# One block product of the values in the head, kept in HBM, and the second chunk of projections whole

## The chip, the cores and the metric

The kernel runs on one core of a Trainium2 chip. Its time is the device time of one execution in microseconds (us); a kernel's figure is the median of several runs. The program is float32 throughout: every product is made of three matrix products of parts in fp32r (the operand is split into a high part and a low part, and high x high, high x low and low x high are added up in one PSUM bank). The engines are PE (matrix products and transposes), ACT, DVE and POOL (elementwise work), and SP, which here only issues transfers.

## The reference

One layer for 512 tokens of 1024 features:

```
xn = RMSNorm(x);  u = xn @ W_in          # columns: q | k | v | rnn_x | rnn_gate | gate_A | gate_B
ya = chunked_band_attention(q, k, v) @ W_attn_out       # 16 heads of 64, chunks of 64, 9 chunks in reach
xc = causal_conv4(rnn_x);  hr = rg_lru(xc)              # two block-diagonal gates, a scan over the tokens
yb = (hr * gelu(rnn_gate)) @ W_rnn_out
h  = x + (sigmoid(gate_A) * ya + sigmoid(gate_B) * yb) @ W_o
h  = h + (silu(g) * up) @ W_ffn_out,  (g | up) = RMSNorm(h) @ W_ffn_in;  out = RMSNorm(h)
```

What the change touches is `rnn_gate` for the first 256 features (chunk `gr0` of `W_in`) and the values `v = xn @ W_v`.

## The kernel before, in words

**Chunks.** The projections run over chunks of 256 columns of `W_in` (`xr0`, `gr0`, `ga0`, `gb0`, `xr2` and so on: rnn_x, rnn_gate, gate_A, gate_B), each for all 512 tokens, as two column tiles of 128 (c = 0, 1) by 8 feature blocks (k = 0 to 7) by three matrix products. A chunk's weights come as two raw tiles of 512 KB (feature blocks 0 to 3 and 4 to 7), and ACT makes the high part (L86, or L670 in the head) and DVE the low part (L87, L671) into tiles named `whl_...`. Raw tiles have three buffers, `whl` tiles four; a new tile waits until the one before it in its buffer has been read for the last time. `prefetch` makes the next chunk's parts in the order of the list `chunks`.

**The head.** The head works in two halves of the tokens. For the first half, DVE and ACT scale the rows, PE transposes them (`turned`, L652, tiles `pt_mix...`), ACT and DVE make the high and the low part of `xnT`, and PE makes the first half of the tokens of `xr0` (`first_half`, products of 128x256) as the blocks arrive. Then comes a fill: the first half of the tokens of `gr0`. While PE works on it, ACT and DVE scale the second half's rows. Then the second half's transposes follow, and with them the second half of the tokens of `xr0` and of `gr0`. Here the order on ACT, DVE and POOL is the order of the code; the order on PE and of the transfers is chosen by a scheduler when the program is built, and fixed then.

**The values.** `v_all` makes the values as a 2 x 2 block product in seven products instead of eight: halves of the tokens by halves of the features, with sums of weight blocks (`t1` to `t4`) and of token blocks (`s1` to `s4`). Each product is 2 banks by 4 feature blocks by 3, so 24 matrix products of 128x512. `x_`, `z_` and `y_` are pairs of PSUM banks. On PE the order is that of the code: `w11` into `x_`, `t1` into `z_`, `t2` onto `x_`, `w22` onto `z_`, `t3` onto `x_`, `w21` into `y_`, `t4` onto `x_`. In between, ACT copies bank contents to SBUF (`keep`, L1025), DVE adds a bank to a kept sum (`summed`, L1035), and ACT and DVE split the sum into the tiles that attention reads (`given`). `t4` = `w21` minus the second sum of weights; it is made when `w21` comes (L310). ACT and DVE here take the scheduler's order.

Of the kernel before, what the change touches and what calls it, by code (L numbers as in the profile page):

```python
# [8 lines left out]
F32 = mybir.dt.float32  # L9
# [5 lines left out]
P = 128  # L15
D = 1024
S = 512
# [25 lines left out]
def block_kernel(ctx: ExitStack, tc: tile.TileContext, x, norm_mix_g, w_in, b_merge, rel_table,  # L43
# [68 lines left out]

    v_groups = ((0, 3), (1, 2))

    v_kinds = ("w11", "t1", "t2", "w22", "t3", "w21", "t4")
    plan_qk(0)
    plan_qk(1)
    for j in range(0, KT, 2):
# [11 lines left out]
        plan(f"o_{kind}")  # L130
    f_units = [f"f{w}{n}" for n in range(3) for w in "gu"]
    f_first = ("w11", "w21", "t4", "t1", "t2", "w22", "t3")
    for unit in f_units:
        for kind in f_first if unit == f_units[0] else v_kinds:
            plan(f"{unit}_{kind}")

    plain, paired = list(range(N_PLAIN)), list(range(N_PLAIN, FT // 2))
# [24 lines left out]
    def load(name, k):  # L162
        _, parts, rows, kts = chunks[index[name]]
        wide = sum(width for *_, width in parts)
        n = min(4 * CW // wide, kts - k)
        at = rows + k * P
        raw = out_raw_home(name) if name[:2] == "fo" else wp.tile([P, n, wide], F32, tag="raw", bufs=3, name=f"raw_{name}_{k}")
        to = 0
        for src, col, width in parts:
            sp.dma_start(out=raw[:, :, to:to + width],  # L170
                         in_=src[at:at + n * P, col:col + width].rearrange("(k p) e -> p k e", p=P))
            to += width
        raws[name, k] = raw
# [122 lines left out]
    def v_weights(kind):  # L296

        hl = [wp.tile([P, 2, 2, S], F32R, tag="whl", bufs=4, name=f"whl_v_{kind}_{u}") for u in range(2)]
        for u in range(2):
            if kind == "t1":  # L300
                src = v_t1[u]
            elif kind in ("t2", "t4"):
                src = v_t2[u]
            elif kind == "t3":
                src = v_raw(kind, 0, 0, u)
                tc.keep_in_program_order(dve.tensor_sub(src, v_t2[u], src))
            else:
                src = v_raw(kind, int(kind[1]) - 1, int(kind[2]) - 1, u)
                if kind == "w21":
                    dve.tensor_sub(v_t2[u], src, v_t2[u])  # L310
            split(hl[u][:, 0], hl[u][:, 1], src)
        return lambda part, k: hl[k // 2][:, part, k % 2]

# [174 lines left out]
    load("xr0", 4)  # L488
    for t in range(2, NT):
        sp.dma_start(out=xt[t][:], in_=x[t * P:(t + 1) * P, :])  # L490
    load("gr0", 0)

    wrg_raw = nm.tile([P, 8, 2, 64], F32, name="wrg_raw")
    for n, w in enumerate((w_rg_r, w_rg_i)):
# [185 lines left out]
    def first_half(name, ks):  # L680
        for c in range(2):
            if (name, c) not in first:
                first[name, c] = mm_tile(f"po_{name}_{c}")
        for k in ks:
            for c in range(2):
                at = slice(c * P, (c + 1) * P)
                whl = made[index[name]]
                mm3(first[name, c][:, 0:256], whl(0, k, at), whl(1, k, at),
                    xnT[k][:, 0, 0:256], xnT[k][:, 1, 0:256], k == 0, k == KT - 1)


# [7 lines left out]
    with tc.manual_schedule(engines={mybir.EngineType.Activation, mybir.EngineType.DVE, mybir.EngineType.Pool}):  # L699
        xs, rs = scaled_first(0)  # L700
        xr0 = chunk_in_parts("xr0")
        xr0(0, 2, dve)
        act.copy(gm[:], gm_p[:, 0:8])
        turned(0, xs, 0)
        first_half("xr0", range(0, 2))
        scaled_rest(0, xs, rs)
        xr0(2, 2, dve)
        turned(0, xs, 2)
        first_half("xr0", range(2, 4))
        xr0(4, 2, dve)  # L710
        turned(0, xs, 4)
        first_half("xr0", range(4, 6))
        gr0 = chunk_in_parts("gr0")
        xr0(6, 2, dve)
        turned(0, xs, 6)
        first_half("xr0", range(6, 8))
        gr0(0, 4, dve)
        first_half("gr0", range(0, 4))
        gr0(4, 4, dve)
        xs, rs = scaled_first(1)  # L720
        gate_weights()
        turned(1, xs, 0)
        first_half("gr0", range(4, 8))
        scaled_rest(1, xs, rs)
        turned(1, xs, 2)
        vectors()
        sp2, spm4 = softplus_neg()
        turned(1, xs, 4)
        turned(1, xs, 6)


    ext = nm.tile([HEADS, 640], F32, tag="junk", bufs=1, name="ext")
# [274 lines left out]

    def v_all(sums):
        out, parted, s, s3 = sums
        x_, y_ = ([mm_tile(f"v_{n}{a}", tag) for a in range(2)] for n, tag in (("x", "mm"), ("y", "t")))  # L1010
        z_ = [mm_tile(f"v_z{a}") for a in range(2)]

        def product(banks, kind, rows, start):
            w = weights(f"v_{kind}")
            for a in range(2):
                for k in range(4):
                    if isinstance(rows, str):
                        hi, lo = (o[:, k, a * P:(a + 1) * P] for o in out[rows])
                    else:
                        hi, lo = (x_block(*rows, part)[:, k, a * P:(a + 1) * P] for part in range(2))  # L1020
                    mm3(banks[a][:], hi, lo, w(0, k), w(1, k), start and k == 0, k == 3, parts=True)

        def keep(o, banks):
            for a in range(2):
                act.activation(o[:, a], banks[a][:], AF.Copy)  # L1025

        def given(half, side, src):
            for a in range(2):
                for n, gr in enumerate(v_groups[side]):
                    v = vs[gr][2 * half + a]  # L1030
                    split(v[:, :, 0::3], v[:, :, 1:3], src(a)[:, n * CW:(n + 1) * CW].rearrange("p (a b d) -> p a b d", a=2, b=2))

        def summed(o, banks, half, side):
            for a in range(2):
                dve.tensor_add(o[:, a], banks[a][:], o[:, a])  # L1035
            for gr in v_groups[side]:
                v_pairs(gr, half)
            given(half, side, lambda a: o[:, a])

        product(x_, "w11", (0, 0), True)  # L1040
        keeps = [rnp.tile([P, 2, 2, S], F32, tag="big", bufs=4, name=f"v_keep{n}") for n in range(2)]
        v_big.append(rnp.tile([P, 2, 2, S], F32R, tag="big", bufs=4, name="v_big"))
        x1, x2, z1 = keeps[0][:, 0], keeps[0][:, 1], keeps[1][:, 0]
        keep(x1, x_)
        product(z_, "t1", "s1", True)
        keep(z1, z_)
        parted("s4", s)
        product(x_, "t2", "s2", False)
        keep(x2, x_)
        parted("s3", s3)  # L1050
        product(z_, "w22", "s4", False)
        summed(x2, z_, 0, 1)
        product(x_, "t3", "s3", False)
        summed(z1, x_, 1, 1)
        product(y_, "w21", (0, 1), True)
        summed(x1, y_, 0, 0)
        product(x_, "t4", (1, 1), False)
        for gr in v_groups[0]:
            v_pairs(gr, 1)
        given(1, 0, lambda a: x_[a][:])  # L1060
# [694 lines left out]
```

## Time and profile before

| | |
|---|---|
| median of 3 runs | 845.96 us (845.82 to 846.02) |
| profiled execution | 846.07 us, span 844.3 us, so 1.77 us lie outside the span |
| PE busy | 836.0 us of the span (99%) |
| DVE, ACT, POOL busy | 657.9, 521.5, 152.4 us |
| stage of the head (start of the span to the first product of `ga0`) | 0 to 36.1 us |
| stage of the values (`w11` to `t4`) | 242.2 to 280.3 us |

In the rows of a timeline the first number is the start, the second the duration, and a bracket gives the engine's idle time before and what ended it. Neighbouring matrix products overlap in the record, so what one costs in a row of them is the distance between starts. Names in the rows have lost their numbers: `po_xr` stands for `xr0` in the head.

### The profile page before, as it was taken

How to read it: one execution, taken by the hardware profiler on the slowest of the kernel's cores; microseconds unless marked ns; L12 is line 12 of the kernel's file. 1: busy time of each engine (PE TensorE's matmuls, PEld its weight loads, DVE VectorE, ACT ScalarE, POOL GpSimd, SP SyncE). 2: the span in 40 equal slices, each digit the busy share in tenths (PEclk: the TensorE clock that was granted, in tenths of full speed). 3: DMA queues.
4: the chain of work that ended last, by engine and by line, in shares of the span. 5: the costliest groups of instructions: out<-in, count | busy, mean ns of one | idle time of the engine just before them, and what ended most of it. 6: DMA issues, size and time to landing. Idle time of an engine off the chain costs nothing.

```text
span 844.3 us, 11949 instructions
## 1 busy us (share of the span) xinstructions
PE 836.0 (99%) x4246; PEld 708.5 (84%) x4246; DVE 657.9 (78%) x960; ACT 521.5 (62%) x862; POOL 152.4 (18%) x207
## 2 busy tenths in 40 slices
PE   9999999999999999999999999999999999999996
PEld 6988888888888888888888888888888999988885
DVE  6688778887959778787568767888777878998784
ACT  7496858774356688878544559663764465455553
POOL 2412030221010043433212000005102321200000
PEclk9999999999999999999999999999999999999998
DMA  8467487653645444548458974565955576644442
GB/s 284 167 222 231 146 302 250 183 203 109 203 151 149 138 145 140 172 134 222 90 134 216 327 287 158 158 181 169 235 176 155 146 189 188 211 151 149 157 168 99
DMA packets 107324, 153.98 MB, mean 182 GB/s; under 512 B 8217, under 2 KB 66161, under 8 KB 106753
## 3 DMA queue, kind: packets, MB, share of 16 engines
q1 hardware_dynamic: 102304, 141.32, 51.7%
q0 software_dynamic: 3728, 8.96, 6.3%
q10 hardware_dynamic: 1232, 2.95, 0.9%
q8 instruction: 33, 0.54, 0.3%
q14 instruction: 27, 0.21, 0.1%
HBM read 139.53 MB, written 30.45 MB: 201 GB/s over the span
## 4 chain that ended last, share of the span: by engine, by line
PE 98%; DVE 1%; ACT 1%; issue 0%; ACTq 0%; DVEq 0%
PE fu_x L82 2%; PE fu_x L81 2%; PE fu_x L80 2%; PE o L1125 2%; PE fg_x L82 2%; PE fg_x L80 2%; PE fg_x L81 2%; PE pT L1105 2%; PE po_gb L80 2%; PE po_xr L81 2%; PE po_xr L80 2%; PE po_ga L82 2%; PE po_ya L80 2%; PE po_k L80 2%; PE po_q L80 2%; PE po_gb L81 2%
## 5 line engine op out<-in xcount | busy, mean ns | idle before, releaser
L1346 POOL TENSOR_TENSOR sg<-sg,keep_fu_x 128x512 f32<-128x512 f32 x8 | 15.6, 1958 | 157.5 <-ACT whl_fu_w L86 108.7
L1089 ACT ACTIVATE p<-p,m 128x128 f32<-128x128 f32 (+1 forms) x64 | 35.5, 556 | 10.2 <-DVE m L1088 9.9
L1094 POOL TENSOR_SCALAR p<-p,rl 128x128 f32<-128x128 f32 (+3 forms) x61 | 38.4, 646 | 17.0 <-DVE rl L1090 12.7
L1088 DVE CUSTOM_DVE_ANT_0 p<-s,bias 128x128 f32<-128x128 f32 (+1 forms) x64 | 28.7, 486 | 13.2 <-PE s L1080 11.5
L87 DVE TENSOR_TENSOR whl_fu_w<-raw_fu_w,whl_fu_w 128x1024 fp32r<-128x1024 f32 (+1 forms) x18 | 22.8, 1270 | 8.7 <-ACT whl_fu_w L86 8.5
L87 DVE TENSOR_TENSOR whl_fu_t<-t_fu,whl_fu_t 128x1024 fp32r<-128x1024 f32 (+1 forms) x18 | 24.2, 1358 | 5.5 <-ACT whl_fu_t L86 5.5
L87 DVE TENSOR_TENSOR pp<-pT,pp 128x384 fp32r<-128x384 f32 (+1 forms) x48 | 26.9, 595 | 2.1 <-ACT pp L86 1.8
L81 PE MATMUL po_xr<-xnT,whl_xr 128*128 128x512 f32 (+1 forms) x80 | 27.7, 353 | 0.0
L81 PE MATMUL po_gr<-xnT,whl_gr 128*128 128x512 f32 (+1 forms) x80 | 27.5, 347 | 0.0
L82 PE MATMUL po_gr<-xnT,whl_gr 128*128 128x512 f32 (+1 forms) x80 | 27.3, 347 | 0.0
L82 PE MATMUL po_xr<-xnT,whl_xr 128*128 128x512 f32 (+1 forms) x80 | 27.2, 346 | 0.0
L80 PE MATMUL po_gr<-xnT,whl_gr 128*128 128x512 f32 (+1 forms) x80 | 27.1, 347 | 0.0
L80 PE MATMUL po_xr<-xnT,whl_xr 128*128 128x512 f32 (+1 forms) x80 | 26.3, 351 | 0.4 <-ACT xnT L654 0.4
L743 POOL MEMSET bias<- 64x64 f32 x16 | 2.3, 146 | 134.1 <-DMA bias<-ext_d 134.0
L86 ACT ACTIVATE whl_fu_w<-raw_fu_w 128x1024 fp32r<-128x1024 f32 (+1 forms) x18 | 17.7, 987 | 13.9 <-issue 7.6
L80 PE MATMUL po_k<-xnT,whl_qk 128*128 128x512 f32 x64 | 25.5, 398 | 0.0
L80 PE MATMUL po_q<-xnT,whl_qk 128*128 128x512 f32 x64 | 25.5, 398 | 0.0
L80 PE MATMUL po_ga<-xnT,whl_ga 128*128 128x512 f32 x64 | 25.5, 398 | 0.0
L80 PE MATMUL po_gb<-xnT,whl_gb 128*128 128x512 f32 x64 | 25.2, 394 | 0.0
L82 PE MATMUL po_ga<-xnT,whl_ga 128*128 128x512 f32 x64 | 25.0, 391 | 0.1
L81 PE MATMUL po_ga<-xnT,whl_ga 128*128 128x512 f32 x64 | 25.0, 390 | 0.0
L81 PE MATMUL po_q<-xnT,whl_qk 128*128 128x512 f32 x64 | 24.9, 390 | 0.0
(689 smaller groups left out, 3083.6 us busy)
## 6 DMA issues: line engine op xcount, KB each, us to landing
raw_qk<-in_w_in_dram SPq DMA_DIRECT2D x32, 256.0 KB, 3.2
out_t<-in_w_ffn_out_dram SPq DMA_DIRECT2D x16, 512.0 KB, 5.6
raw_fu_w<-in_w_ffn_in_dram SPq DMA_DIRECT2D x16, 512.0 KB, 4.7
raw_fo<-in_w_ffn_out_dram SPq DMA_DIRECT2D x14, 512.0 KB, 4.1
raw_t<-out_t SPq DMA_DIRECT2D x24, 256.0 KB, 3.7
raw_xr<-in_w_in_dram SPq DMA_DIRECT2D x8, 512.0 KB, 5.9
raw_gr<-in_w_in_dram SPq DMA_DIRECT2D x8, 512.0 KB, 4.5
raw_ga<-in_w_in_dram SPq DMA_DIRECT2D x8, 512.0 KB, 5.5
```

Of the source, the lines that this page charges most:

```text
L80: pe.matmul(o, sh, mh, start=start, stop=False, skip_group_check=parts)
L81: pe.matmul(o, sh, ml, start=False, stop=False, skip_group_check=parts)
L82: pe.matmul(o, sl, mh, start=False, stop=stop, skip_group_check=parts)
L86: act.activation(hi, src, AF.Copy)
L87: dve.tensor_sub(lo, src, f(hi))
L743: pool.memset(b[64:128, 448:512], NEG)
L1088: dve.tensor_tensor_reduce(prob[qb][:], scs[qb][:, 0:w], bias[:, S - w:S], -1.0, 3e38, ALU.add, ALU.min, nmax[:, qb:qb + 1])
L1089: act.activation(prob[qb][:], prob[qb][:], AF.Exp, bias=nmax[:, qb:qb + 1], scale=-1.0, accum_out=lsum[:, qb:qb + 1])
L1094: eng.tensor_scalar(prob[qb][:], prob[qb][:], rl[:, qb:qb + 1], 1.0, ALU.mult, ALU.mult)
L1105: pe.transpose(pt[:, at * P:(at + 1) * P], prob[qb][:, kb * P:(kb + 1) * P], ident[:])
L1125: pe.matmul(po[:, S - n:S], st, pp[i][:, part, lo:lo + n], start=kb == 0 and part == 0, stop=kb == NT - 1 and part == 1)
L1346: (pool if keep and (unit != f_units[-1] or side) else dve).tensor_mul(o, o, keep_ if keep else bank)
```

## The change

- In the head the fill is no longer the first half of the tokens of `gr0`. It is the `w21` product of the values (token block 0, features 512 to 1023, the 24 matrix products of 128x512), made in two parts (`vy_weights`, `vy_product`) into the banks `v_y0` and `v_y1`. Its weights are loaded where the first half of `gr0` was.
- After the second half's transposes, ACT copies the two banks to an SBUF tile, SP writes it to HBM (`vy_d`, 512 KB), and then the parts of `gr0`'s weights are made. `gr0` is multiplied once, for all 512 tokens.
- In `v_all` the product `w21` is gone. The kept product is read back from HBM into the place of the first kept sum, and DVE adds the banks of `w11` to it, which replaces ACT's copy of them. `t4` loads the block `w21` of the weights itself, and follows `t3` directly on PE.

```diff
-    v_kinds = ("w11", "t1", "t2", "w22", "t3", "w21", "t4")
+    v_kinds = ("w11", "t1", "t2", "w22", "t3", "t4")
...
+            elif kind == "t4":
+                dve.tensor_sub(v_t2[u], v_raw(kind, 1, 0, u), v_t2[u])
+                src = v_t2[u]
...
-    load("gr0", 0)
+    vy_raw = [v_raw("y", 1, 0, 0)]
...
+    vy_d = dr.tile([P, 2, S], F32, name="vy_d")
+    def vy_weights(u):
+        if u:
+            vy_raw.append(v_raw("y", 1, 0, u))
+        hl = wp.tile([P, 2, 2, S], F32R, tag="whl", bufs=4, name=f"whl_vy_{u}")
+        split(hl[:, 0], hl[:, 1], vy_raw[u])
+        vy_hl.append(hl)
+    def vy_product(u):
+        if not vy:
+            vy.extend(mm_tile(f"v_y{a}") for a in range(2))
+        for a in range(2):
+            for k in range(2):
+                x_ = xnT[4 + 2 * u + k][:, :, a * P:(a + 1) * P]
+                mm3(vy[a][:], x_[:, 0], x_[:, 1], vy_hl[u][:, 0, k], vy_hl[u][:, 1, k], u == k == 0, u == k == 1)
...
         first_half("xr0", range(6, 8))
-        gr0(0, 4, dve)
-        first_half("gr0", range(0, 4))
-        gr0(4, 4, dve)
+        vy_weights(0)
+        vy_product(0)
+        vy_weights(1)
         xs, rs = scaled_first(1)
         gate_weights()
         turned(1, xs, 0)
-        first_half("gr0", range(4, 8))
+        vy_product(1)
         scaled_rest(1, xs, rs)
...
         turned(1, xs, 6)
+        vy_tile = nm.tile([P, 2, S], F32, name="vy_tile")
+        for a in range(2):
+            act.activation(vy_tile[:, a], vy[a][:], AF.Copy)
+        sp.dma_start(out=vy_d[:], in_=vy_tile[:])
+        prefetch(index["gr0"] + 1)
...
-        x1, x2, z1 = keeps[0][:, 0], keeps[0][:, 1], keeps[1][:, 0]
-        keep(x1, x_)
+        y1, x2, z1 = keeps[0][:, 0], keeps[0][:, 1], keeps[1][:, 0]
+        sp.dma_start(out=y1, in_=vy_d[:])
+        for a in range(2):
+            dve.tensor_add(y1[:, a], x_[a][:], y1[:, a])
...
         summed(z1, x_, 1, 1)
-        product(y_, "w21", (0, 1), True)
-        summed(x1, y_, 0, 0)
+        given_all(y1, 0, 0)
         product(x_, "t4", (1, 1), False)
```

Outside the head and the values the five engines' orders are the same in both programs.

**PE, in the middle of the second half's transposes.** Before, the transposes `pt_mix1_4...` stand among products of two chunks, `xr0` and `gr0`:

```order
L80 MATMUL po_xr0_0_218<-xnT_179,whl_xr0_0_203 128x256 [waits Activation_49]
L80 MATMUL po_xr0_1_219<-xnT_179,whl_xr0_0_203 128x256
L80 MATMUL po_gr0_0_310<-xnT_179,whl_gr0_0_282 128x256
L80 MATMUL po_gr0_1_311<-xnT_179,whl_gr0_0_282 128x256
L652 MATMUL pt_mix1_4s_449<-ident_143,xs_mix2_340 128x128 [waits DVE_49,PE_49]
```

In the changed program only `xr0` is left between them, and `gr0` comes behind the last of `xr0`:

```order
L654 MATMUL pt_mix1_6t_437<-ident_143,xs_mix3_332 128x128
L80 MATMUL po_xr0_0_220<-xnT_180,whl_xr0_4_206 128x256 [waits Activation_49]
L80 MATMUL po_xr0_1_221<-xnT_180,whl_xr0_4_206 128x256
L81 MATMUL po_xr0_0_220<-xnT_180,whl_xr0_4_206 128x256 [waits DVE_49]
...
L80 MATMUL po_gr0_0_553<-xnT_180,whl_gr0_0_451 128x512 [waits Activation_49]
L81 MATMUL po_gr0_0_553<-xnT_180,whl_gr0_0_451 128x512
L80 MATMUL po_gr0_1_578<-xnT_180,whl_gr0_0_451 128x512
L81 MATMUL po_gr0_1_578<-xnT_180,whl_gr0_0_451 128x512
L82 MATMUL po_gr0_0_553<-xnT_180,whl_gr0_0_451 128x512 [waits DVE_49]
```

So 48 products of `gr0` left the stretch of the transposes, and what follows the transposes starts with weights that ACT and DVE make last.

**ACT, behind the last high parts of the second half** (changed program):

```order
L656 ACTIVATE xnT_180<-pt_mix1_6t_437,gm_179 128x256 [waits PE_49]
L656 ACTIVATE xnT_180<-pt_mix1_6s_438,gm_179 128x256
L753 ACTIVATE vy_tile_447<-v_y0_311 128x512
L753 ACTIVATE vy_tile_447<-v_y1_312 128x512
L86 ACTIVATE whl_gr0_0_451<-raw_gr0_0_452 128x1024 [waits DMAHW0_49]
L86 ACTIVATE whl_gr0_4_456<-raw_gr0_4_457 128x1024 [waits DMAHW1_49]
L783 ACTIVATE xc0_530<-po_xr0_0_220,vc_181 128x512 [waits PE_49]
```

Before, `xc0` followed the high parts directly; the two copies and the two weight parts are new there.

**DVE, from the second part of `t3` on.** Before:

```order
L87 TENSOR_TENSOR whl_v_t3_1_2383<-raw_v_t3_001_2390,whl_v_t3_1_2383 128x1024 [waits Activation_49]
L310 TENSOR_TENSOR v_t2_1_2159<-raw_v_w21_101_2439,v_t2_1_2159 128x1024 [waits DMAHW6_49,DMAHW5_49]
L87 TENSOR_TENSOR whl_v_w21_0_2431<-raw_v_w21_100_2433,whl_v_w21_0_2431 128x1024 [waits Activation_49]
L1035 TENSOR_TENSOR v_keep0_2299<-v_z1_2268,v_keep0_2299 128x512 [waits PE_49]
L87 TENSOR_TENSOR v_big_2301<-v_keep0_2299,v_big_2301 128x2x128 [waits Activation_49]
L87 TENSOR_TENSOR v2_0_2422<-v_keep0_2299,v2_0_2422 128x2x128 [waits Activation_49]
L87 TENSOR_TENSOR whl_v_w21_1_2432<-raw_v_w21_101_2439,whl_v_w21_1_2432 128x1024 [waits Activation_49]
L1035 TENSOR_TENSOR v_keep1_2300<-v_x0_2263,v_keep1_2300 128x512 [waits PE_49]
```

and now:

```order
L309 TENSOR_TENSOR v_t2_1_2154<-raw_v_t4_101_2433,v_t2_1_2154 128x1024 [waits DMAHW4_49,DMAHW3_49]
L87 TENSOR_TENSOR whl_v_t4_0_2425<-v_t2_0_2045,whl_v_t4_0_2425 128x1024 [waits Activation_49]
L1061 TENSOR_TENSOR v_keep0_2292<-v_z1_2261,v_keep0_2292 128x512 [waits PE_49]
L87 TENSOR_TENSOR v_big_2294<-v_keep0_2292,v_big_2294 128x2x128 [waits Activation_49]
L87 TENSOR_TENSOR v2_0_2416<-v_keep0_2292,v2_0_2416 128x2x128 [waits Activation_49]
L87 TENSOR_TENSOR v0_0_2474<-v_keep0_2292,v0_0_2474 128x2x128 [waits Activation_49] x2
L87 TENSOR_TENSOR v3_0_2475<-v_keep0_2292,v3_0_2475 128x2x128 [waits Activation_49] x2
L1061 TENSOR_TENSOR v_keep1_2293<-v_x0_2258,v_keep1_2293 128x512 [waits PE_49]
L87 TENSOR_TENSOR whl_v_t4_1_2426<-v_t2_1_2154,whl_v_t4_1_2426 128x1024 [waits Activation_49]
L87 TENSOR_TENSOR v_big_2294<-v_keep0_2292,v_big_2294 128x2x128 [waits Activation_49]
L87 TENSOR_TENSOR v2_0_2416<-v_keep0_2292,v2_0_2416 128x2x128 [waits Activation_49]
L87 TENSOR_TENSOR whl_qk2_0_2484<-raw_qk2_0_2485,whl_qk2_0_2484 128x1024 [waits DMAHW6_49,DMAHW5_49,Activation_49]
```

directly followed by `v_keep1<-v_x1`. The two parts of `w21` became parts of `t4`; the four splits of the kept product (`v0_0`, `v3_0`) now stand ahead of the first read of the banks of `t3` (`v_keep1<-v_x0`), and four more rows ahead of the second (`v_keep1<-v_x1`).

More of the change, by code (lines that the diff above doesn't have):

```diff
@@ L132, in block_kernel @@
     f_first = ("w11", "w21", "t4", "t1", "t2", "w22", "t3")
+    f_kinds = ("w11", "t1", "t2", "w22", "t3", "w21", "t4")
     for unit in f_units:
-        for kind in f_first if unit == f_units[0] else v_kinds:
+        for kind in f_first if unit == f_units[0] else f_kinds:
             plan(f"{unit}_{kind}")
@@ L301, in v_weights @@
                 src = v_t1[u]
-            elif kind in ("t2", "t4"):
+            elif kind == "t2":
                 src = v_t2[u]
@@ L306, in v_weights @@
                 tc.keep_in_program_order(dve.tensor_sub(src, v_t2[u], src))
+            elif kind == "t4":
+                dve.tensor_sub(v_t2[u], v_raw(kind, 1, 0, u), v_t2[u])
+                src = v_t2[u]
             else:
                 src = v_raw(kind, int(kind[1]) - 1, int(kind[2]) - 1, u)
-                if kind == "w21":
-                    dve.tensor_sub(v_t2[u], src, v_t2[u])
             split(hl[u][:, 0], hl[u][:, 1], src)
@@ L689, in first_half @@
                     xnT[k][:, 0, 0:256], xnT[k][:, 1, 0:256], k == 0, k == KT - 1)
+    vy_hl, vy = [], []
+    vy_d = dr.tile([P, 2, S], F32, name="vy_d")
[12 more added lines that the diff above has]
+                mm3(vy[a][:], x_[:, 0], x_[:, 1], vy_hl[u][:, 0, k], vy_hl[u][:, 1, k], u == k == 0, u == k == 1)
     wrg = rw2.tile([P, 2, 8, P], F32R, bufs=1, name="wrg")
@@ L712, in block_kernel @@
         first_half("xr0", range(4, 6))
-        gr0 = chunk_in_parts("gr0")
         xr0(6, 2, dve)
@@ L1009, in v_all @@
         out, parted, s, s3 = sums
-        x_, y_ = ([mm_tile(f"v_{n}{a}", tag) for a in range(2)] for n, tag in (("x", "mm"), ("y", "t")))
+        x_ = [mm_tile(f"v_x{a}") for a in range(2)]
         z_ = [mm_tile(f"v_z{a}") for a in range(2)]
@@ L1035, in summed, with given_all @@
                 dve.tensor_add(o[:, a], banks[a][:], o[:, a])
+            given_all(o, half, side)
+        def given_all(o, half, side):
             for gr in v_groups[side]:
```

## The prediction

> **What bounds the kernel now.** I read the page first, then the waits of PE, then the timelines of PE, ACT and DVE in the two stages that the change touches.
>
> ```profile
> PE 836.0 (99%) x4246; PEld 708.5 (84%) x4246; DVE 657.9 (78%) x960; ACT 521.5 (62%) x862; POOL 152.4 (18%) x207
> PE 98%; DVE 1%; ACT 1%; issue 0%; ACTq 0%; DVEq 0%
> PE po_xr L80 <- ACT xnT L654: 0.4, 2, 0.2
> ```
>
> PE is the bound nearly everywhere: it holds 98% of the chain that ended last, and apart from the start its longest wait for another engine, the one in the third row, sums to 0.4 us. So a microsecond taken off PE's row of products is a microsecond of time, and so is one in which PE waits; what ACT, DVE or transfers do counts only where PE comes to wait for it. No later stage has slack on PE that could swallow a delay. Sums are made against the profiled execution, 846.07 us; the median of the runs is 0.11 us below it.
>
> **The change part by part.** *Products moved and products made wide.*
>
> ```profile
> 16.48 0.28 PE L80 MATMUL po_gr<-xnT,whl_gr 128*128 128x256 f32 x1
> 22.24 0.27 PE L652 MATMUL pt_mix_0t<-ident,xs_mix 128*128 128x128 f32 x1
> 60.10 0.39 PE L80 MATMUL po_xr<-xnT,whl_xr 128*128 128x512 f32 x1
> 70.98 0.39 PE L80 MATMUL po_gr<-xnT,whl_gr 128*128 128x512 f32 x1
> 269.39 0.39 PE L80 MATMUL v_y<-whl_v_w,xnT 128*128 128x512 f32 x1
> 274.83 0.39 PE L80 MATMUL v_x<-whl_v_t,xnT 128*128 128x512 f32 x1
> ```
>
> Between the first two rows lie the 48 half products of the fill: 5.76 / 48 = 0.120 us each. Between the next two lie 48 whole ones: 10.88 / 48 = 0.2267. The last two bracket the 24 of `w21`: 5.44 us. These 24 go from the values to the head, +5.44 and -5.44, nothing in the sum. `gr0` costs 96 x 0.120 = 11.52 before and 48 x 0.2267 = 10.88 after: **-0.64**. By the Trainium skill, page "TensorE: Matmul & The Clock Gate", section "Back-to-back issue gap", a matmul of N columns takes N / 2.4 + 2.5 ns after another. An estimate from that page: two halves 218.3 ns, one whole 215.8, so 48 pairs would give 0.12 us instead of 0.64, and the whole sum would come out 0.5 higher; the rows here differ from the page and I go by the rows.
>
> *The fill.* It becomes 24 x 0.2267 = 5.44 instead of 5.76 us, so the second half's transposes start at 21.92 instead of 22.24, if the scaled rows are there. Does the fill's own input come in time?
>
> ```profile
> 16.36 1.06 ACT L670 ACTIVATE whl_gr<-raw_gr 128x1024 fp32r<-128x1024 f32 x1 [1.12 <-DMA raw_gr<-in_w_in_dram]
> 17.45 1.23 DVE L671 TENSOR_TENSOR whl_gr<-raw_gr,whl_gr 128x1024 fp32r<-128x1024 f32 x1 [0.96 <-ACT whl_gr L670]
> 20.39 0.49 DVE L632 TENSOR_SCALAR xs_mix<-x,rs_mix 128x512 f32<-128x512 f32 x1
> ```
>
> The second raw tile landed at 16.36 and its low part was done at 18.68; PE reaches the second part of the fill at 16.48 + 12 x 0.2267 = 19.2. The new load has the same 512 KB in two transfers, in the same place of SP's queue. It may be half a microsecond later and still cost nothing. The scaled rows were done at 20.88, a microsecond ahead.
>
> *The stretch of the transposes.*
>
> ```profile
> 23.52 0.50 PE L80 MATMUL po_xr<-xnT,whl_xr 128*128 128x256 f32 x2 [0.24 <-ACT xnT L654]
> 36.10 0.40 PE L80 MATMUL po_ga<-xnT,whl_ga 128*128 128x512 f32 x1
> 26.13 1.28 ACT L576 ACT_TABLE_LOAD   x1
> 27.42 0.21 ACT L576 ACTIVATE sp_e<-sp_al 128x8 f32<-128x8 f32 x1
> 27.71 0.48 ACT L654 ACTIVATE xnT<-pt_mix_4t,gm 128x256 fp32r<-128x256 f32 x1
> 29.01 0.47 ACT L654 ACTIVATE xnT<-pt_mix_6s,gm 128x256 fp32r<-128x256 f32 x1
> 28.22 0.48 DVE L656 SCALAR_TENSOR_TENSOR xnT<-pt_mix_4t,gm,xnT 128x256 fp32r<-128x256 f32 x1
> ```
>
> Before, PE had 96 half products to lay between the transposes, and from 23.52 to 36.10 it never stopped. Now it has 48. ACT's chain sets when blocks 4 to 7 arrive: the table load and `sp_e` keep it until 27.63, so in the changed order the high part of block 4 comes at 27.6 - 0.3 + 0.48 = 27.8 and its low part (DVE, a half microsecond behind, as the last row shows) at 28.3. PE's work until then, from 23.2, is the first 24 products (2.9), eight transposes (0.9, at 0.11 each) and `vp` (0.1), and a short wait of 0.1 at `vp`: done at 27.35. It waits 0.5 for the high and 0.25 for the low part; then 22 products of 0.12 end at 31.0.
>
> *`gr0`'s weights.* They are now made behind the transposes.
>
> ```profile
> 255.99 0.60 ACT L1025 ACTIVATE v_keep<-v_x 128x512 f32<-128x512 f32 x1 [0.45 <-PE v_x L82]
> 14.19 1.05 ACT L670 ACTIVATE whl_gr<-raw_gr 128x1024 fp32r<-128x1024 f32 x1
> 15.27 1.22 DVE L671 TENSOR_TENSOR whl_gr<-raw_gr,whl_gr 128x1024 fp32r<-128x1024 f32 x1 [0.28 <-ACT whl_gr L670]
> 36.80 0.40 PE L81 MATMUL po_ga<-xnT,whl_ga 128*128 128x512 f32 x1
> 37.26 0.50 PE L82 MATMUL po_ga<-xnT,whl_ga 128*128 128x512 f32 x1
> ```
>
> ACT ends the last high part about 28.8, then two bank copies (0.5 apart, as 0.60 with the overlap) to 29.8, then the high part until 30.85, DVE's low part from there 1.22: 32.1. PE comes at 31.0, does four products with the high part (0.9), waits 0.25, and the other 44 take 9.97: `gr0` ends at 42.1. Without waits it would be 36.10 + 5.44 - 0.64 = 40.9. So the new waits in the head are **+1.2**. Their cover is the 48 products that are gone. If ACT and DVE are 0.3 quicker at block 4, 0.7 of it stays; if the weight part is later, see the rivals. Bounds: 0.4 to 2.3. The next chunk had a wait of 0.23 between the last two rows (0.46 apart instead of 0.23), for its low part; that part now has five more microseconds: **-0.2**. The write to HBM and the loads behind it in SP's queue (weights of `ga0` and `gb0`, blocks of `W_o`) fall in that gain of time; I cost them at nothing. The read back is queued by 240 at the earliest and needed at about 245; 256 KB transfers there land in about 3 us.
>
> *The values.* `t4` goes onto the banks of `t3`, so its first product waits until DVE has read `x0`, its thirteenth until it has read `x1`. The 5.44 us of `w21` between hid that; DVE was late there already:
>
> ```profile
> 258.50 1.23 DVE L87 TENSOR_TENSOR whl_v_t<-raw_v_t,whl_v_t 128x1024 fp32r<-128x1024 f32 x1 [0.86 <-ACT whl_v_t L86]
> 261.35 1.23 DVE L310 TENSOR_TENSOR v_t<-raw_v_w,v_t 128x1024 f32<-128x1024 f32 x1 [0.50 <-DMA raw_v_w<-in_w_in_dram]
> 262.49 0.69 DVE L1035 TENSOR_TENSOR v_keep<-v_z,v_keep 128x512 f32<-128x512 f32 x1
> 263.09 1.22 DVE L87 TENSOR_TENSOR whl_v_t<-raw_v_t,whl_v_t 128x1024 fp32r<-128x1024 f32 x1
> 264.23 1.22 DVE L310 TENSOR_TENSOR v_t<-raw_v_w,v_t 128x1024 f32<-128x1024 f32 x1
> 265.36 1.22 DVE L87 TENSOR_TENSOR whl_v_w<-raw_v_w,whl_v_w 128x1024 fp32r<-128x1024 f32 x1
> 266.50 0.69 DVE L1035 TENSOR_TENSOR v_keep<-v_z,v_keep 128x512 f32<-128x512 f32 x1
> 267.10 0.42 DVE L87 TENSOR_TENSOR v_big<-v_keep,v_big 128x256 fp32r<-128x256 f32 x1
> 267.43 0.42 DVE L87 TENSOR_TENSOR v<-v_keep,v 128x256 fp32r<-128x256 f32 x1
> 267.76 1.22 DVE L87 TENSOR_TENSOR whl_v_w<-raw_v_w,whl_v_w 128x1024 fp32r<-128x1024 f32 x1
> 268.90 0.69 DVE L1035 TENSOR_TENSOR v_keep<-v_x,v_keep 128x512 f32<-128x512 f32 x1
> ```
>
> From 261.35, where a load releases it, DVE is not idle; by the distances of starts a row of 128x1024 costs 1.14, one of 128x512 0.60, one of 128x256 0.33. In the order of the changed program the rows down to 267.43 keep their times (a part of `t4` stands for one of `w21`). From 267.76 come four splits of the kept product, 4 x 0.33, then the read of `x0` at 269.1, done at 269.8. PE ends `t3` at 269.39: **wait 0.45**. Twelve products later, at 272.6, it wants `x1`. DVE until then: a part of `t4` (1.14), two splits (0.67), a part of `qk2` (1.14), so the read of `x1` starts at 272.65 and ends at 273.35: **wait 0.8**. Together **+1.25**; bounds 0.4 (everything from 261.35 on half a microsecond earlier, and the part of `qk2` not needed there yet) to 2.4 (that part late by its own length). Behind `t4` the transposes of attention need nothing new, and DVE has nearly eight microseconds until the first product with the values.
>
> Sum: -0.64 + 1.2 - 0.2 + 1.25 = **+1.6**, so 847.7 for a profiled execution and 847.5 for the median. That is +0.19%; what a measurement here can tell from no change is about 0.2%, 1.7 us, so this stands just inside it.
>
> **The rivals.** *DVE slowed by POOL at `gr0`'s low part* (slower). The low part of `ga0` shows it: 2.31 us beside 1.22 for the same shape, while POOL ran a 128x512 subtraction.
>
> ```profile
> L87 DVE TENSOR_TENSOR whl_ga<-raw_ga,whl_ga x2: 1217/1764/2311, 36.0 to 37.1; 128x1024 fp32r<-128x1024 f32 x2
> 36.88 1.47 POOL L769 TENSOR_TENSOR xch<-xc,xch 128x512 fp32r<-128x512 f32 x1 [2.01 <-ACT xch L768]
> ```
>
> `gr0`'s low part falls beside POOL's softplus chain (small rows of 0.2 us, 28.2 to 34.9). If each costs as much, PE waits 1.1 longer: 848.6. Against it: those rows are 128x8. The Trainium skill, page "GPSIMD Engine Reference", section "Specifications", has the two engines share their SBUF interfaces and contend when a DVE instruction has two inputs there; a low part has. The trace agrees with that at `ga0`.
>
> *The read of `t3` later still* (slower). The load that releases DVE at 261.35, or the part of `qk2` that now stands ahead of `x1`, comes 1 to 2 us later: 849. Against it: the transfers around it are no more than before, one read of 512 KB apart.
>
> *No wait in the values*: DVE's rows run 1.3 us earlier, say by an early load: 846.3. *No new wait anywhere* (faster), with every wait covered, -0.64 - 0.2: 845.1. Against both: DVE's chain from 258.50 starts with PE's own release of a buffer, and the order of its rows is fixed.
>
> **How the numbers follow.** Forecast 0.50, its own range 846.7 to 848.4; POOL 0.15; a later read 0.12; no wait in the values 0.13; no new wait 0.10. The forecast's half above 847.65 counts as slower: 0.24 + 0.15 + 0.12, about 0.50. Its other half, and both cases without waits but for their fast end, are within 0.2%: 0.45. Faster than 844.3 nothing here reaches by itself: 0.05. The range that leaves out two in ten goes from 845.6 to 849.3.
>
> **What would show it.** In the changed profile: the transposes at about 21.9; `po_gr` in 48 products of 128x512, first at 31.0, with waits of PE on ACT and DVE before it that sum to about 1.2 more; `po_ga` at 42.1. In the values, PE's first `t4` product 0.4 and its thirteenth 0.8 behind, waiting for `v_keep<-v_x`; from `w11` to the first attention transpose 33.9 instead of 38.1 us. The prediction is wrong if PE never waits at `t4`, if `po_ga` starts before 41.3 or after 43.2, or if a product elsewhere waits for the read back or for a load behind the write.

## The result, and the profile after

The changed kernel took 849.04 us at the median of six runs beside 846.08 us for the kernel before in the same session. One of the six, a slow run, took 4811 us; without it the median is 848.92, the ratio 1.0033, and its 95% interval 1.0022 to 1.0043. It is slower by about 2.8 us, which is more than the 0.2% that counts here as no change. The prediction's time was 847.5 us, its range 845.6 to 849.3, its chance of slower 0.50. The result lies near the upper end of that range, and above the 846.7 to 848.4 that the forecast itself had.

The waits of PE in the changed kernel (line and tile that waited, engine waited for: us in total, times, longest); the last row stood in the profile before too:

```profile
PE v_x L80 <- DVE v_keep L1061: 1.8, 2, 1.4
PE pt_mix_0t L654 <- DVE xs_mix L634: 0.6, 2, 0.4
PE po_xr L80 <- ACT xnT L656: 0.4, 2, 0.2
```

The first row is new and the largest: the products of `t4` wait for DVE's reads of `t3`'s banks. The page shows it from its other end: the chain that ended last, 98% PE before, now leaves PE for the load of `t4`'s weights and DVE's rows behind it, from 263.0 to 280.0 us (and for some rows of the head).

```profile
PE 836.4 (99%) x4198; PEld 705.6 (83%) x4198; DVE 660.3 (78%) x960; ACT 519.6 (61%) x862; POOL 152.9 (18%) x207
PE 94%; DVE 3%; DMA 1%; ACT 1%; issue 0%; POOL 0%; SPq 0%; ACTq 0%; DVEq 0%; POOLq 0%
```

The busy time of PE is no guide: it rose by 0.4 us although 0.64 us of products are gone and waits were added, because a product behind a wait reads longer (0.47 and 0.50 us below, where the others read 0.39). Times have to be taken from the starts of rows. PE's timeline of the changed kernel, the rows at which one stretch ends and the next begins, with the rows in the values at which PE is held up:

```profile
16.10 0.63 PE L80 MATMUL v_y<-whl_vy,xnT 128*128 128x512 f32 x2
21.60 0.27 PE L654 MATMUL pt_mix_0t<-ident,xs_mix 128*128 128x128 f32 x1
30.67 0.40 PE L80 MATMUL po_gr<-xnT,whl_gr 128*128 128x512 f32 x1
41.81 0.39 PE L80 MATMUL po_ga<-xnT,whl_ga 128*128 128x512 f32 x1
247.48 0.39 PE L80 MATMUL v_x<-whl_v_w,xnT 128*128 128x512 f32 x1
270.60 0.39 PE L80 MATMUL v_x<-whl_v_t,v_s3h 128*128 128x512 f32 x1
270.99 0.50 PE L81 MATMUL v_x<-whl_v_t,v_s3h 128*128 128x512 f32 x1
274.79 0.39 PE L82 MATMUL v_x<-whl_v_t,v_s3l 128*128 128x512 f32 x1
276.56 0.47 PE L80 MATMUL v_x<-whl_v_t,xnT 128*128 128x512 f32 x1 [1.39 <-DVE v_keep L1061]
280.01 0.50 PE L80 MATMUL v_x<-whl_v_t,xnT 128*128 128x512 f32 x1 [0.45 <-DVE v_keep L1061]
282.88 1.25 PE L1135 MATMUL pT<-ident,p 128*128 128x128 f32 x10
```

With the same rows of before (and the first gate product `rg`, at 47.50 before and 52.78 after), the 3.20 us between the two profiled executions (849.27 and 846.07) fall apart so:

| stretch on PE, us | before | change | difference | predicted |
|---|---|---|---|---|
| start to the fill's first product | 16.48 | 16.10 | -0.38 | 0 |
| fill, to the second half's first transpose | 5.76 | 5.50 | -0.26 | -0.32 |
| to the first `po_ga` | 13.86 | 20.21 | +6.35 | +6.32 |
| `ga0`, to the first gate product | 11.40 | 10.97 | -0.43 | -0.2 |
| to `w11` of the values | 194.69 | 194.70 | +0.01 | 0 |
| `w11` to attention's first transpose | 38.09 | 35.40 | -2.69 | -4.2 |
| to the end of the span | 564.02 | 564.62 | +0.60 | 0 |

The head up to `po_ga` came out as worked out, to a tenth. The values gave back 2.7 us instead of 4.2. They are where the forecast was short.

DVE's timeline of the changed kernel there:

```profile
264.92 1.22 DVE L307 TENSOR_TENSOR raw_v_t<-v_t,raw_v_t 128x1024 f32<-128x1024 f32 x1
267.98 1.23 DVE L309 TENSOR_TENSOR v_t<-raw_v_t,v_t 128x1024 f32<-128x1024 f32 x1 [1.84 <-DMA raw_v_t<-in_w_in_dram]
269.72 1.22 DVE L87 TENSOR_TENSOR whl_v_t<-raw_v_t,whl_v_t 128x1024 fp32r<-128x1024 f32 x1
273.12 0.68 DVE L1061 TENSOR_TENSOR v_keep<-v_z,v_keep 128x512 f32<-128x512 f32 x1
274.06 1.76 DVE L87 TENSOR_TENSOR v<-v_keep,v 128x256 fp32r<-128x256 f32 x5
275.73 0.68 DVE L1061 TENSOR_TENSOR v_keep<-v_x,v_keep 128x512 f32<-128x512 f32 x1
278.14 1.22 DVE L87 TENSOR_TENSOR whl_qk<-raw_qk,whl_qk 128x1024 fp32r<-128x1024 f32 x1
279.27 0.68 DVE L1061 TENSOR_TENSOR v_keep<-v_x,v_keep 128x512 f32<-128x512 f32 x1
```

The order of rows is the one that the prediction used: the read of `x0` (275.73) stands behind the splits of the kept product, the read of `x1` (279.27) behind a part of `qk2`. But the whole row of work starts late. Before, DVE waited 0.50 us for the load at this place; here it waits 1.84 us. Counted from the values' start, the row with that wait comes at 267.98 - 247.48 = 20.50 instead of 261.35 - 242.19 = 19.16: 1.34 us late, and DVE has no idle time behind it to make that up. The lateness costs PE at a third place too, which the list of waits does not show: the low part of `t3`'s second weights (269.72) now ends at 270.94, and PE's products at 270.60 and 270.99 stand 0.39 and 0.34 us from the next, 0.28 more than two common distances.

### The profile page after: what moved, and what is told of

The parts are those of the page before. It is cut to its first block, busy times and chain, and to the rows that moved or that the text cites. A ratio compares the mean times of both kernels' runs of the same rounds, so it can differ in the third digit from the quotient of the medians.

```text
span 847.5 us, 11862 instructions
## 1 busy us (share of the span) xinstructions
PE 836.4 (99%) x4198; PEld 705.6 (83%) x4198; DVE 660.3 (78%) x960; ACT 519.6 (61%) x862; POOL 152.9 (18%) x207
## 4 chain that ended last, share of the span: by engine, by line
PE 94%; DVE 3%; DMA 1%; ACT 1%; issue 0%; POOL 0%; SPq 0%; ACTq 0%; DVEq 0%; POOLq 0%
PE fu_x L82 2%; PE fu_x L81 2%; PE fu_x L80 2%; PE fg_x L81 2%; PE fg_x L82 2%; PE fg_x L80 2%; PE o L1155 2%; PE pT L1135 2%; PE po_gb L80 2%; PE po_ga L80 2%; PE po_gr L82 2%; PE po_q L80 2%; PE po_k L80 2%; PE po_ya L80 2%; PE po_ga L82 2%; PE po_ga L81 2%
## 5 line engine op out<-in xcount | busy, mean ns | idle before, releaser
L1376 POOL TENSOR_TENSOR sg<-sg,keep_fu_x 128x512 f32<-128x512 f32 x8 | 13.6, 1695 | 159.7 <-DVE keep_fu_x L1375 159.7
L86 ACT ACTIVATE whl_fu_t<-t_fu 128x1024 fp32r<-128x1024 f32 (+1 forms) x18 | 17.5, 986 | 13.9 <-PE fu_x L82 9.2
L80 PE MATMUL po_k<-xnT,whl_qk 128*128 128x512 f32 x64 | 25.5, 398 | 0.0
L82 PE MATMUL po_gr<-xnT,whl_gr 128*128 128x512 f32 x64 | 25.0, 391 | 0.0
L81 PE MATMUL po_k<-xnT,whl_qk 128*128 128x512 f32 x64 | 24.9, 390 | 0.0
```

The source lines that it names most:

```text
L80: pe.matmul(o, sh, mh, start=start, stop=False, skip_group_check=parts)
L81: pe.matmul(o, sh, ml, start=False, stop=False, skip_group_check=parts)
L82: pe.matmul(o, sl, mh, start=False, stop=stop, skip_group_check=parts)
L86: act.activation(hi, src, AF.Copy)
L1376: (pool if keep and (unit != f_units[-1] or side) else dve).tensor_mul(o, o, keep_ if keep else bank)
```

## The experiments

Three questions were asked: is the loss in the values, what sets the wait at `t4`, and why did that load come late? Then the head's waits were tried, and versions with the repairs. All times are medians, and the kernel before took 846.1 to 846.3 us in these sessions. The stretches are read from PE's timelines as above (us).

| kernel | median | ratio to before, 95% | fill | transposes to `po_ga` | `w11` to attention | rest |
|---|---|---|---|---|---|---|
| before | 846.1 | | 5.76 | 13.86 | 38.09 | 564.02 |
| change | 849.04 | 1.0022 to 1.0043 | 5.50 | 20.21 | 35.40 | 564.62 |
| change, again | 849.57 | 1.0024 to 1.0051 | 5.48 | 20.19 | 35.29 | 564.17 |
| head alone | 852.37 | 1.0057 to 1.0083 | 5.66 | 20.21 | 38.08 | 564.62 |
| 48 matmuls at the start | 848.16 | 1.0014 to 1.0032 | 5.80 | 20.18 | 34.03 | 564.44 |
| 16 matmuls at the start | 847.91 | 1.0015 to 1.0036 | 7.04 | 20.20 | 33.92 | 564.15 |
| reads first | 847.53 | 1.0011 to 1.0029 | 5.65 | 20.24 | 33.21 | 564.16 |
| `w22` as cover | 846.53 | 1.0001 to 1.0019 | 5.47 | 20.20 | 32.64 | 564.25 |
| softplus late | 848.84 | 1.0025 to 1.0049 | 5.48 | 19.85 | 35.36 | 564.31 |
| cover and softplus | 846.46 | 0.9998 to 1.0016 | 5.99 | 19.84 | 32.65 | 566.83 |
| `gr0` early | 848.39 | 1.0020 to 1.0045 | 5.48 | 19.24 | 35.27 | 564.19 |
| cover and `gr0` early | 846.20 | 0.9988 to 1.0006 | 5.48 | 19.25 | 32.64 | 565.38 |

**The head alone.** The product is made in the head as in the change, but the values are those of the kernel before:

```diff
-    v_kinds = ("w11", "t1", "t2", "w22", "t3", "t4")
+    v_kinds = ("w11", "t1", "t2", "w22", "t3", "w21", "t4")
...
-        given_all(y1, 0, 0)
+        product(y_, "w21", (0, 1), True)
+        summed(x1, y_, 0, 0)
         product(x_, "t4", (1, 1), False)
```

> The head of the changed kernel with the values of the kernel before: the product `w21` is made in the head and written to HBM as in the change, but not read back; the values make it again between `t3` and `t4`, which costs 24 x 0.2267 = 5.44 us more of PE than the change. Theory (the loss lies in the values, where nothing covers DVE's reads of `t3`): no wait at `t4`, `w11` to the first transpose of attention 38.1 us as before; the head costs 5.44 - 0.64 + 1.3 - 0.4 more than before, so 851.6 to 852.0. Rival (the loss lies in the head, or in later stages that the read back or the queue disturb): 853 or more, with waits of PE outside the head.

Measured: 852.37 us, 0.4 above what the theory expected. (The product is written to HBM and not read back.) The values take 38.08 us, as before to a hundredth, with no wait at `t4`; the head takes what it takes in the change to 0.2 us. What is over lies in the last stretch, which is 0.60 us longer than in the profile of the kernel before. So the head's share of the loss is the one predicted, and the rest of it needs the missing products between `t3` and `t4`.

**`w22` as cover.** The products between `t3` and `t4` are put back, by changing the order of two blocks:

```diff
-    v_kinds = ("w11", "t1", "t2", "w22", "t3", "t4")
+    v_kinds = ("w11", "t1", "t2", "t3", "w22", "t4")
...
-        product(z_, "w22", "s4", False)
-        summed(x2, z_, 0, 1)
         product(x_, "t3", "s3", False)
         summed(z1, x_, 1, 1)
+        product(z_, "w22", "s4", False)
+        summed(x2, z_, 0, 1)
```

> The changed kernel with `t3` ahead of `w22` in the values, so that the 24 products of `w22` (5.44 us, on other banks) lie between `t3` and `t4` as those of `w21` did before. Same products, loads and splits. Theory (the loss is the missing cover between `t3` and `t4`): no wait at `t4`, `w11` to the first transpose of attention 32.7 to 33.0 us (6 x 5.44 = 32.6), 2.5 to 2.8 us less than the change: 846.2 to 846.6. Rivals: `t3`'s weights or the copy of `x1` by ACT are now late (a wait moved to `t3`'s start, 847 to 849); or the loss is not there at all (849).

Measured: 846.53 us, and 32.64 us for the values, which is 6 x 24 products at 0.2267 and nothing else. This run's list of waits no longer has a row for `v_x`, and `t4` follows `w22` at the common pitch:

```profile
PE busy L480 <- DVE eps_t L486: 1.2, 1, 1.2
PE pt_mix_0t L654 <- DVE xs_mix L634: 0.4, 2, 0.3
PE po_xr L80 <- ACT xnT L656: 0.4, 2, 0.2
...
274.38 0.39 PE L82 MATMUL v_z<-whl_v_w,v_s4l 128*128 128x512 f32 x1
274.61 0.39 PE L80 MATMUL v_x<-whl_v_t,xnT 128*128 128x512 f32 x1
```

The same products in another order take away all of the loss in the values, 35.40 - 32.64 = 2.8 us, and neither rival showed. The load of `t4`'s first half was late here too (DVE waited 0.60 us for it) and cost nothing.

**Reads first.** Only DVE's queue is changed: the four splits of the kept product go behind the two reads.

```diff
-                dve.tensor_add(o[:, a], banks[a][:], o[:, a])
+                reads.append(dve.tensor_add(o[:, a], banks[a][:], o[:, a]))
...
-        given_all(y1, 0, 0)
+        with tc.issue_after(reads[-1].ins): given_all(y1, 0, 0)
         product(x_, "t4", (1, 1), False)
```

> The changed kernel with the four splits of the kept product `y1` put behind DVE's two reads of `t3`'s banks (same work, another order on DVE and ACT). Theory (DVE's queue sets the wait at `t4`): the read of `x0` comes 4 x 0.33 = 1.3 us earlier, PE's first wait at `t4` falls from 1.4 to 0.1 to 0.3 us, the second one, for `x1`, stays within 0 to 0.5 since a part of `qk2` still stands ahead of it; 847.0 to 847.6. If the wait comes from something else than the order of DVE's rows (a DMA that gates the read itself), waits and time stay at 849.0.

Measured: 847.53 us, 33.21 us for the values. Of the two waits at `t4` one is left, at the thirteenth product, where the part of `qk2` still stands ahead of the read (PE's waits in this run):

```profile
PE v_x L80 <- DVE v_keep L1061: 0.3, 1, 0.3
```

Not all of the gain is the order's. Counted from the values' start, the read of `x0` came 2.2 us earlier than in the change: 1.3 for the four splits, and 0.8 because the load that DVE waits for landed after 3.6 us in this execution, where it took 4.4 in the change. The size of the first part is that of the four rows, so DVE's queue in front of the reads sets the wait, as the prediction had it, together with the load that starts the row.

**The late load.** The load that DVE waited for moves the same bytes from the same place as the load of `w21` before, and it was issued at the same distance from its neighbours. What differs stands in the list of DMA queues. The five microseconds from 0.5 us ahead of its issue, before and after, and the time from its two issues to their landing (min/median/max, us):

```profile
q1 hardware_dynamic: 867, 0.84, 57.4%
DMA to landing us min/median/max: 2.9/3.0/3.2
```

```profile
q1 hardware_dynamic: 877, 0.85, 56.9%
q8 instruction: 1, 0.02, 1.4%
q14 instruction: 1, 0.01, 0.4%
DMA to landing us min/median/max: 4.3/4.4/4.5
```

In the change there is a transfer of 16 KB on queue q8, of kind "instruction", in the middle of it: 1.4% of 16 engines over 5 us is 1.1 us on one of them. The page counts 33 such transfers in either kernel; the next one in the change comes 29 us later, which is 128 products at 0.2267 us. If they are PE's own instructions, their place is set by the number of matmuls ahead, and the change has fewer of them ahead: 48 in the whole kernel, of which 24 are missing in front of the values (`w11` starts behind 1146 matmuls instead of 1170), since `w21` now stands there. That can be tried without touching anything else: the start of the kernel has 16 warming products during which PE has nothing else to do.

```diff
-    for _ in range(16):
-        pe.matmul(busy[:], idle[:, 0:P], idle[:], start=True, stop=True)
+    for _ in range(64):
+        pe.matmul(busy[:, 0:128], idle[:, 0:P], idle[:, 0:128], start=True, stop=True)
```

> The changed kernel with the 16 warming products of 512 columns at the very start made as 64 of 128 columns: 48 matmuls more in PE's stream, at a place where PE waits anyway, so that PE stands at the same count of instructions in front of the values as in the kernel before. The 16 KB instruction transfers of queue q8 should all come 48 products (about 11 us) earlier, the one at 264.0 at about 253. Theory A (that transfer, 1.16 us on one DMA engine, holds up the load of `t4`'s first half, which landed 4.4 us after its issue instead of 3.1 before): the load lands after about 3.1 us, PE's first wait at `t4` falls from 1.4 to about 0.3, and the time from 849.0 to about 847.8. Theory B (the load is late by itself, or DVE's order alone sets the wait): landing, waits and 849.0 stay.

PE does not stand at the count of the kernel before in front of the values, as this has it, but at 1194 matmuls, 24 more.

Measured: 848.16 us, where about 847.8 was expected. The transfer came at 252 instead of 264. The window around the same load, its landing, and DVE's row that waits for it:

```profile
q1 hardware_dynamic: 897, 0.87, 60.9%
q14 instruction: 1, 0.01, 0.5%
DMA to landing us min/median/max: 2.9/3.0/3.2
267.07 1.23 DVE L309 TENSOR_TENSOR v_t<-raw_v_t,v_t 128x1024 f32<-128x1024 f32 x1 [0.48 <-DMA raw_v_t<-in_w_in_dram]
```

The load lands after 3.0 us, DVE waits 0.48 us as it did before the change, and the values take 34.03 us: 1.38 us over the bare products, where the prediction had 1.25. The small transfer on queue q14 is in this window too, so it is not what delays the load.

> The changed kernel once more, unaltered, beside the three below. Theory A (PE's instruction transfer falls into the load of `t4`'s first half in every execution, since both have their place in the program): that transfer comes again near 264, the load lands 3.5 to 4.5 us after its issue (3.1 before, 3.0 with the transfer moved away), PE waits 1.9 to 2.8 us between `t3`'s first product and attention's first transpose (1.4 with it moved away), and the time is 848.5 to 849.2. Theory B (the late load was chance in one execution): landing at 3.0 to 3.2 us, 848.0.

Measured: 849.57 us, 0.4 above the expected range. The transfer is again at 264, the load lands after 4.3 us, the waits at `t4` are again 1.9 us: not chance.

The second dose had 32 products of 256 columns at the start, 16 matmuls more than the change:

> The changed kernel with the 16 warming products made as 32 of 256 columns: 16 matmuls more in PE's stream, so that the 16 KB instruction transfer near 264 should come 16 x 0.2267 = 3.6 us earlier, near 260.5. There it meets the load of `t3`'s second half (issued near 259.5, landed after 2.9 us), which has about a microsecond to spare. Theory A: that load lands after 3.5 to 4.2 us, the load of `t4`'s first half after 3.0 to 3.2, PE's waits in the values are about 1.4 us as with 48 matmuls, and the time 847.8 to 848.3. Theory B (the number of matmuls at the start does something else, say at the start itself): landings unmoved, 849 or the start visibly shifted.

Measured: 847.91 us, with the transfer at 260.8 and the load of `t4`'s first half landing after 2.9 us, 33.92 us for the values. It did not hit the load of `t3`'s second half as expected: it started 0.6 us ahead of that load's issue (261.4), and the load landed after 3.1 us. Counted from the values' start it had moved by 5.6 us against the change, where 16 products are 3.6. In this execution everything from the head on was also 1.6 us late, transfer and load alike: the fill's second weight tile had landed late and PE waited twice for it (PE's timeline there):

```profile
19.79 0.73 PE L80 MATMUL v_y<-whl_vy,xnT 128*128 128x512 f32 x2 [0.46 <-ACT whl_vy L86]
21.05 0.50 PE L81 MATMUL v_y<-whl_vy,xnT 128*128 128x512 f32 x1 [0.53 <-DVE whl_vy L87]
```

Counted in matmuls, the place of this transfer, the tenth on q8, is the same in all twelve profiles: it starts behind 1213 to 1222 of them (1214 before, 1222 in the change, 1214 and 1213 with 48 and 16 more at the start). So it follows PE's stream, to within 9 products or 2 us.

Over all kernels with the transfer beside this load (nine profiles, the head-alone kernel's load of `w21` among them) it landed 3.6 to 4.4 us after its issue at the median; in the three without (before, 48, 16) after 2.9 to 3.0. In the head-alone kernel the same delay (DVE waited 1.07 us there) cost nothing, because `w21` lay between.

The Trainium skill, page "Runtime: NRT & Kernel Launch", section "Instruction fetch mechanics", says that each engine's instructions are streamed in blocks of 16 KiB, 256 instructions, by a DMA queue of its sequencer, and that crossing a boundary is "mostly hidden". The size and the distance agree with the rows here (128 products are 256 instructions when each has its weight load); what it does to a load beside it, 0.6 to 1.4 us, is not hidden where a stage hangs on that load.

**The head's waits.** First the softplus of the recurrence, with its table load on ACT, is put behind the transposes and `gr0`'s weights:

```diff
-        sp2, spm4 = softplus_neg()
         turned(1, xs, 4)
         turned(1, xs, 6)
...
         prefetch(index["gr0"] + 1)
+        sp2, spm4 = softplus_neg()
```

> The changed kernel with the softplus of the recurrence (on ACT an absolute value, a table load of 1.28 us and an exponential) put behind the last transposes, the copies of the kept product and `gr0`'s weights. Theory (the head's new waits come from that table load ahead of block 4 of the normalized rows, and from `gr0`'s weights made late behind it): from the second half's first transpose to `po_ga` 19.1 to 19.4 us instead of 20.2, that is 0.8 to 1.1 less; 848.0 to 848.3. Rival (the head is paced by the eviction of the transposes or by something else): 20.0 to 20.2 us and 849. A third way: the softplus chain on POOL, now some 8 us later, comes too late for the recurrence's first gates at 52.8, and the gain comes back as a wait there.

Measured: 19.85 us from the transposes to `po_ga` instead of 20.2, a third of what was expected, and 848.84 us. The recurrence's first gates did not wait for the later softplus: from `po_ga` to the first gate product it took 10.97 us as in the change. ACT's timeline of this run (the high part of block 4; block 6; `gr0`'s weights):

```profile
25.74 0.48 ACT L656 ACTIVATE xnT<-pt_mix_4t,gm 128x256 fp32r<-128x256 f32 x1 [1.10 <-PE pt_mix_4t L654]
27.37 0.47 ACT L656 ACTIVATE xnT<-pt_mix_6t,gm 128x256 fp32r<-128x256 f32 x1 [0.80 <-PE pt_mix_6t L654]
29.06 2.02 ACT L86 ACTIVATE whl_gr<-raw_gr 128x1024 fp32r<-128x1024 f32 x2
```

Block 4 came 1.3 us earlier and PE's wait for it went. But ACT now waited for PE's transposes of block 6, so `gr0`'s weights were hardly earlier, and PE, earlier by 0.6, waited longer for them. The wait had moved one step on. So in the next run the first half of `gr0`'s weights goes into ACT's idle time of 1.10 us ahead of block 4:

```diff
+        gr0 = chunk_in_parts("gr0")
+        gr0(0, 4, dve)
         turned(1, xs, 4)
         turned(1, xs, 6)
...
-        prefetch(index["gr0"] + 1)
+        gr0(4, 4, dve)
+        sp2, spm4 = softplus_neg()
```

> The changed kernel with softplus behind the transposes as in `soft_late`, and also the first half of `gr0`'s weights made ahead of the transposes of blocks 4 and 5, where ACT stood idle for 1.10 us and DVE for 0.91 in that run. Theory (in `soft_late` the gain at block 4, 0.6 us, was partly given back because PE came earlier to weights that were no earlier): the gaps before `gr0`'s third to fifth product go, and from the second half's first transpose to `po_ga` it takes 19.2 to 19.4 us instead of 19.85 (20.2 in the change); 0.9 below the change: 848.1 to 848.6. Rival: PE's rows in the head are paced by block 6's transposes and evictions, 19.6 or more.

Measured: 19.24 us and 848.39 us. The head's new waits are 1.23 us: 6.35, less the 5.12 by which 48 whole products take longer than 48 halves. So 0.97 of them was this: the table load ahead of block 4, and weights made behind it.

**Both repairs.** `w22` as cover together with the one and then the other head:

> Both repairs on the changed kernel: `t3` ahead of `w22` in the values, softplus behind the transposes in the head. Theory: the gains add, 846.5 - 1.0 = 845.5, 0.6 under the kernel before (the change's own 0.64 for the whole chunk and 0.4 at `ga0`, with some 0.4 left of waits). If the head's gain comes back at the gates: 846.5.

> `gr0_early` with `t3` ahead of `w22` in the values as in `w22_cover`. Theory: the two gains add, 846.5 - 0.9 = 845.6, some 0.5 below the kernel before. If the jitter of loads and of POOL's rows that showed up in single executions hides that: 846.0 to 846.5, no difference from before.

Measured: 846.46 and 846.20 us, the second 0.9988 to 1.0006 of the kernel before: no difference, 1.0 and 0.6 us above what the sums of the gains gave. The transposes and the values took what they should (the rows of the table), and in the second kernel attention began 0.86 us earlier than before (279.42 against 280.28). In its profiled execution that was lost again at the start of the output projection. The chain of waits there:

```profile
466.85 11.18 DMA h<-in_x_dram
...
478.08 0.52 issue
478.60 0.68 DVE h L1270
479.28 0.61 DVE ms L87
...
479.94 0.50 PE o_z L82
```

A product of the output projection waits for DVE, and DVE for a row block of `x` that is loaded again and lands when it lands, while the DMA engines move 292 GB/s (462 to 479 us). The same stretch of PE is 1.0 us longer here than in the kernel before. Whether that takes the gain in the other executions too was not tried. In the first one's profile PE waited 1.8 us for a row of POOL's in attention that ran 2.2 us instead of about 0.7, and 0.4 at the same place of the output projection; that execution was 3 us above the median.

## Why the prediction was right, and where it was not

- *Products moved and made wide* (0 and -0.64): right. The 48 whole products of `gr0` lie within 11.14 us (30.67 to 41.81), of which 10.88 are 48 x 0.2267 and 0.26 the wait for the low part and what hangs on it. The estimate from the Trainium skill's page, 0.5 more, was not borne out. That section gives the formula for a single matmul, and about 131 ns for 512 columns in a stream with weight loads; here it is 226.7.
- *The head's new waits* (+1.2): right in size and place. From the first transpose to `po_ga` 20.18 us were worked out and 20.21 measured; `po_gr` came 9.07 behind the first transpose (9.08 worked out). The runs with the softplus and `gr0`'s weights moved took 0.97 of it away, so the causes named were the ones.
- *`ga0`'s wait gone* (-0.2): mis-sized, -0.43. Counted was the wait alone. The first product after it (37.26 in the kernel before) also stood 0.34 us from the next instead of 0.227, and the nine behind that 0.235 apart: another 0.2.
- *The write, and the loads behind it* (nothing): right; no row of PE waits for the read back, and the stretch from `ga0` to `w11` has the same length to 0.01. It was close: the read back's 512 KB took 4.6 to 5.8 us to land in all runs that have it, where about 3 had been taken, and in five of them DVE waited for it (0.28 to 1.37 us); PE was not held up by that.
- *The values* (+1.25): mechanism right, size wrong, 2.75, above the bound of 2.4. The step that failed is "the rows down to 267.43 keep their times". It took over from the trace of before that the load which releases DVE lands 3.0 us after its issue; it landed after 4.4, and DVE's row behind it came 1.34 us late. With that load at 2.9 to 3.0 us (48 and 16 matmuls at the start) the loss is 1.38 and 1.28. The other 1.3 to 1.4 us come from PE's instruction transfer, whose place in the values the change moved: 24 matmuls fewer stand ahead of them. That 1.38 and 1.28 are so near to 1.25 is partly luck. The waits themselves were 0.37 and 0.46, and 0.25 and 0.44, where 0.45 and 0.8 had been worked out; what makes up for it is about 0.25 us behind each wait, which the working did not have.
- *The rivals.* "The read of `t3` later still" (849, chance 0.12) is what happened, in its place and size. Against it stood that the transfers around were no more than before; that looked at the data queues and not at the instruction queue. "POOL slows DVE at `gr0`'s low part" did not happen: both low parts took 1.22 us. "The change without new waits" (845.1) would need both repairs, and even then the measured time was 846.2.
- *The start and the last stretch* (0 each): -0.38 and +0.60 in the profiled execution. The fill started at 16.07 to 16.63 in all twelve profiles, so the first is within what executions differ by. Of the second, 0.31 is one wait of a transpose for a row of POOL's in attention (392.35), which the change run again does not have. In the other profiles the last stretch was 0.1 to 0.6 longer than in the one profile of the kernel before, leaving out the two that the repairs' section tells of; why was not settled.

## What to carry to other kernels

Products that change banks are also a cover for the read of the banks before them: when some are taken from between two products on the same banks, look how far the reading engine's queue is behind, and put other work of the same length there (here `w22`, at no cost). A wait that is taken away on one engine shows up at the next thing that was made in its shadow, so move the whole row of what feeds the bound. And a load on which a stage hangs needs room beyond the landing time that one profile shows (here up to 1.4 us): where the instruction transfers fall in a stage changes with the matmuls added or removed ahead of it.

## What the runs showed that had not been expected

- An instruction transfer of 16 KB (about 1.1 us on one DMA engine) that falls beside a load of 512 KB moves its landing from 3.0 us to between 3.6 and 4.4, though the bytes per microsecond around it look the same. The number of matmuls far ahead sets where it falls: 48 more moved it from 264 to 252 us.
- After a wait the first product stands further from the second: 276.56 to 276.87 and 280.01 to 280.35, 0.31 and 0.34 us instead of 0.2267. With the longer distance at its end, each wait costs 0.24 to 0.27 us more than its own figure (1.63 for 1.39, 0.72 for 0.45).
- Where DVE and POOL met in the changed kernel, POOL's rows were the longer ones. DVE's low parts of `gr0` and `ga0` kept 1.22 us, and four of the softplus chain's rows beside them took 1.0 to 1.3 us instead of 0.2 (groups with two of the four, of the changed kernel, then of the kernel before, min/median/max in ns):

```profile
L590 POOL TENSOR_TENSOR sp_p<-sp_p,sp_s x6: 201/202/1022, 28.4 to 33.2; 128x8 f32<-128x8 f32 x6
L591 POOL TENSOR_SCALAR sp_p<-sp_p x6: 231/232/1158, 28.7 to 33.5; 128x8 f32<-128x8 f32 x6
L87 DVE TENSOR_TENSOR whl_gr<-raw_gr,whl_gr x2: 1218/1221/1224, 30.4 to 31.5; 128x1024 fp32r<-128x1024 f32 x2
```

```profile
L588 POOL TENSOR_TENSOR sp_p<-sp_p,sp_s x6: 201/202/203, 29.1 to 32.1; 128x8 f32<-128x8 f32 x6
L589 POOL TENSOR_SCALAR sp_p<-sp_p x6: 231/232/245, 29.4 to 32.4; 128x8 f32<-128x8 f32 x6
```

In the kernel before it was DVE's row that took 2.31 us beside a large row of POOL's. The Trainium skill, page "GPSIMD Engine Reference", section "Specifications", says that the two contend for their SBUF interfaces when a DVE instruction has two inputs there, as a low part has. The rows here show either side taking longer: the small row of POOL beside a large one of DVE, and DVE's beside a large one of POOL.
